# A one-core decoder step: single first blocks, squares through PSUM, a convolution in two chains, a mean from two products, and other groups for transferred lo parts

## Chip, core and metric

The kernel runs on one core of one Trainium2 chip, in one launch. The metric is device time in microseconds (us), the lower the better, given as the median of several executions. The core has a matrix engine (PE), a vector engine (DVE), an activation engine (ACT), a general engine (POOL) and a queue engine (SP) that issues most of the DMA transfers. Each runs its own list of instructions in a fixed order and waits on semaphores for the others.

## What is computed

One layer of a decoder trunk over 288 token columns: 256 of a prompt and 8 requests with 4 new tokens each. The width is 2048, the inner width 8192, everything is float32.

```python
h = rmsnorm(x, norm1_g)
proj = h @ w_in + b_in                      # 2048 -> 3 * 1024
a, gate, z = split(proj)
u = a * sigmoid(gate)
c = silu(layernorm(depthwise_causal_conv(hist_conv ++ u, conv_w) + conv_b))   # 31 taps
d = multiscale_pool(hist_pool ++ z)         # window means of 2, 4, 8, 16, less z
p = (d grouped @ pool_w) * pool_scale       # 4 groups of 256
x = x + concat(c, p) @ w_out
x = x + square(relu(rmsnorm(x, norm2_g) @ w_ff1)) @ w_ff2
y = rmsnorm(x, norm_f)
```

The last 30 values of u and the last 15 of z are outputs as well.

## The kernel before

**Layout and products.** Channels lie on the 128 partitions, tokens along the free axis. Each float32 operand is split into a rounded `hi` and the rest `lo`, and every product is three matmuls of 128x128 by 128x288: hi·hi (L297), hi·lo (L298), lo·hi (L299), in `gemm` (L283). 384 blocks of 128x128 of `w_in`, 16 of the pooling weights, 256 of `w_out` and 2 x 1024 of the feed-forward weights go through it, some 8,100 matmuls in all.

**Weights.** SP loads 512 KB at a time into `wr` (six buffers, L149), one such half being four blocks of rows for 256 columns. `split_part` (L251) makes `whi` on ACT (L257) and `wlo` in one of three ways, named by a letter: V is a subtraction on DVE (L262), G two subtractions on POOL (L265), and D is a negated copy on ACT (L259) followed by a second transfer of the same weights from memory that adds onto it (L260, issued by POOL). The letters of a group come from the table `WAYS` (L70): four letters for the four halves of a convolution tile `c0` to `c7` or of a pooling group `p0` to `p3`. `whi` and `wlo` have five buffers each.

**Order.** `SEQUENCE` (L45) is c0 c1 c2 c3 c4 p3 c5 p2 P3 c6 p1 P2 p0 P1 c7 P0, a capital letter being the small product of a pooling group. Python only fixes dependencies and priorities; a scheduler orders each engine's list from its own timing model. `later()` (L108) lowers the priority of what it encloses, `tc.issue_after(i)` puts an instruction behind another.

**The first stage.** Tiles c0 and c1 go first and together, so that each block of rows of x feeds 12 matmuls. `FIRST` (L183) lists the transfers: blocks 0 and 1 singly, the other 14 in pairs; six entries are issued ahead. For each entry `first_split` (L316) scales x by the gain on ACT, takes its lo part on DVE (L322), and splits the weights (way V). The RMS norm's squares (`squares`, L363) are made between these on ACT into a scratch of five 128x576 pieces in `z_all`, added on DVE (L372 to L374). `first_sums` puts their sum over the partitions (`pt`, L222) in PE's list ahead of block 15, `rsqrt_sums` (L213) takes the root on DVE and ACT, and `first_rows` has PE spread the result (L242) ahead of block 2 of c2.

**Convolution.** `conv_pair` (L392) evicts a tile's two banks into u and then writes, at low priority, the taps: for the prompt ACT makes tap 0 (L412) and DVE adds taps 1 to 30 one on the other in a PSUM tile `pc` (L415), shared by two tiles, the last into `c`. For the samples POOL multiplies all taps (`prd`, L419) and DVE reduces (L421).

**Pooling.** `pool_group` (L429) evicts z, POOL doubles the windows (L444), DVE and POOL take the mean less z (L449, L453), and ACT and DVE split the result `d` into `dx` (L455, L456). `pool_products` (L461) multiplies it and leaves scaled hi and lo parts (L467, L468).

**Layer norm and output.** `w_out` runs eight groups over the pooling half, then eight over the convolution half. Into the first eight are put, by `BETWEEN` (L530): the mean over channels (`ln_mean`, group 4, block 4: DVE adds the last pair of tiles and the two halves, L507 and L508, then one product with `ones`, L510), the squared deviations (`ln_sums`, group 5, block 6) and the rows (`ln_rows`, group 6, block 4). POOL has added the first three pairs before (L424). The outputs of u and z leave by SP at the lowest priority (L500, L501).

Of the kernel before, what the change touches and what calls it, by code (L numbers as in the profile page):

```python
# [69 lines left out]
WAYS = {"c2": "GVGV", "c3": "GDGD", "c4": "GDGD", "p3": "GDDG", "c5": "GDGD", "c": "GGGV", "p": "GVVG", "w": "GG", "ff": "VV"}  # L70
# [13 lines left out]
def trunk_kernel(ctx: ExitStack, tc: tile.TileContext, io):  # L84
# [95 lines left out]
    def first_x(k, n):  # L180
        nc.sync.dma_start(xT[:, k : k + n, :], io["xT"][:, k : k + n, :])
# [4 lines left out]
    for k, n in FIRST[:6]:  # L186
        first_x(k, n)
        if k > 0:
            first_weights(k, n, nc.sync)
# [124 lines left out]
    hx, firsts = [], []  # L314

    def first_split(k0, n):  # L316
        for k in range(k0, k0 + n):
            if k % 2 == 0:
                hx.extend(halves(act2("hx")))
            hh, hl = hx[k]  # L320
            nc.scalar.activation(hh, xT[:, k, :], AF.Copy, scale=v("norm1_g", k))
            nc.vector.scalar_tensor_tensor(out=hl, in0=xT[:, k, :], scalar=v("norm1_g", k), in1=f32(hh), op0=ALU.mult, op1=ALU.subtract)  # L322
# [5 lines left out]

    for j, (k, n) in enumerate(FIRST):
        if j >= 6:  # L330
            first_x(k, n)
            first_weights(k, n, nc.sync)
        first_split(k, n)
# [26 lines left out]
    scratch = z_all[:].rearrange("p k t -> p (k t)")[:, 0 : 5 * 2 * T].rearrange("p (n k t) -> p n k t", n=5, t=T)  # L360
    tot = [scratch[:, 0], scratch[:, 1]]

    def squares():  # L363

        nc.scalar.copy(scratch[:, :, :, 0:1], f32(firsts[0][0])[:, 1, 1, 0:10].rearrange("p (n k t) -> p n k t", n=5, t=1))
        for q in range(8):
            xq = xT[:, 2 * q : 2 * q + 2, :]
            a = q // 4
            dst = scratch[:, 2 + q % 3] if q % 4 else tot[a]
            nc.scalar.activation(dst, xq, AF.Square)  # L370
# [3 lines left out]
        nc.vector.tensor_tensor(tot[0][:, 0, :], tot[0][:, 0, :], tot[0][:, 1, :], op=ALU.add)  # L374
        return [tot[0][:, 0, :]]
# [4 lines left out]
    cs, pcs = [], []  # L380
    sum_c = tmpp.tile([P, 2, T], F32, name="sum_c", tag="ag2", bufs=2)
# [10 lines left out]
    def conv_pair(i, banks):  # L392
# [9 lines left out]
        for out, a, b in ((up[:, CH:UO], ta[:, :SEQ], tg[:, :SEQ]), (us[:, :, CH:US], samples(ta[:, SEQ:T], NS), samples(tg[:, SEQ:T], NS))):  # L402
            nc.vector.scalar_tensor_tensor(out=out, in0=a, scalar=v("b_in", i), in1=b, op0=ALU.add, op1=ALU.mult)
        if i % 2 == 0:
            cs.append(actp.tile([P, 2, T], F32, name=nm("c"), tag="c", bufs=4))
        c = cs[i // 2][:, i % 2, :]
        with later():
            if i % 2 == 0:
                pcs.append(cvp.tile([P, 2, SEQ], F32, name=nm("pc"), tag="cv"))
            pc = pcs[i // 2][:, i % 2, :]  # L410
            cwv = vec[:, CWO + i * CW : CWO + (i + 1) * CW]
            nc.scalar.activation(pc, up[:, 0:SEQ], AF.Identity, bias=v("conv_b", i), scale=cwv[:, 0:1])  # L412
            for w in range(1, CW):
                dst = pc if w < CW - 1 else c[:, 0:SEQ]
                nc.vector.scalar_tensor_tensor(out=dst, in0=up[:, w : w + SEQ], scalar=cwv[:, w : w + 1], in1=pc, op0=ALU.mult, op1=ALU.add)  # L415
# [6 lines left out]
            if i % 2 and 1 < i < N8 - 1:  # L422
                for m in range(2):
                    nc.gpsimd.tensor_tensor(sum_c[:, m, :], (cs[0] if i == 3 else sum_c)[:, m, :], cs[i // 2][:, m, :], op=ALU.add)  # L424
# [65 lines left out]
    conv_pair(1, pair1)  # L490
    conv_pair(2, third)
    for kind, i in SEQUENCE[3:]:
        if kind == "c":
            conv_pair(i, conv_products(i))
        elif kind == "p":
# [195 lines left out]
```

## Time and profile before

| | |
|---|---|
| median of 3 executions | 1104.44 us (1103.78 to 1106.19) |
| the profiled execution | 1105.06 us, of which the span from first to last instruction is 1103.1 us |
| granted PE clock, mean over the span | 0.996 |
| PE busy | 1087.3 us of the span, 8204 instructions |
| DVE, ACT, POOL busy | 638.2, 477.8, 179.1 us |
| HBM read, written | 185.68 MB, 4.28 MB |

The span falls into four stretches: the first stage with its loads (0 to about 31 us), the input projection with convolution and pooling (to about 172 us), the output projection (to about 290 us) and the feed-forward part. In a row of a group stand the line, the engine, what is written and read, the count, then busy time, mean duration in ns, the idle time of the engine ahead of it and what ended it. In a row of the timeline stand start, length, engine, line, operation, shapes, count, and in brackets the engine's idle time ahead of it and what ended that. A length with a count above one is from the first start to the last end. Matmuls overlap each other, so a matmul of 296 ns does not mean one result per 296 ns.

### The profile page before, as it was taken

To read this page: it belongs to the slowest core of one execution; us is meant where nothing else is said; L and a number is where in the kernel's file an instruction comes from. 1 tells how busy PE (TensorE), PEld (TensorE's weight loads), DVE (VectorE), ACT (ScalarE), POOL (GpSimd) and SP (SyncE) were. 2 spreads that over 40 slices of the span, in tenths; PEclk is the share of its full clock that TensorE was granted. 3 is DMA by queue.
4 is the path that set the end of the run, shared out by engine and by line. 5 is a ranking of instruction groups with operands and counts; after the bars stand their busy time and mean duration, and the time that the engine had idled before them with its cause. 6 is when DMAs were issued, how large, how long until landed. Compare 5 with 4: busy or idle time off the path is not lost.

```text
span 1103.1 us, 19716 instructions
## 1 busy us (share of the span) xinstructions
PE 1087.3 (99%) x8204; PEld 1085.0 (98%) x8204; DVE 638.2 (58%) x814; ACT 477.8 (43%) x585; POOL 179.1 (16%) x209
## 2 busy tenths in 40 slices
PE   9999999999999999999999999999999999999996
PEld 8999999999999999999999999999999999999996
DVE  7889999787555444445544444545544445554553
ACT  8654445565544433333443333444433334444441
POOL 0879989512000000000000000000000000000000
PEclk9999999999999999999999999999999999999998
DMA  9996568555555555555555555555555555555522
GB/s 334 279 275 176 155 159 245 168 169 162 166 161 170 168 162 168 171 161 165 170 167 162 171 163 165 171 168 161 169 170 160 168 171 164 165 170 163 164 75 86
DMA packets 58265, 191.24 MB, mean 173 GB/s; under 512 B 6208, under 2 KB 11328, under 8 KB 58176
## 3 DMA queue, kind: packets, MB, share of 16 engines
q1 hardware_dynamic: 56752, 185.53, 53.7%
q0 software_dynamic: 1152, 4.19, 2.1%
q8 instruction: 64, 1.05, 0.4%
q10 hardware_dynamic: 272, 0.26, 0.1%
q14 instruction: 25, 0.20, 0.0%
HBM read 185.68 MB, written 4.28 MB: 172 GB/s over the span
## 4 chain that ended last, share of the span: by engine, by line
PE 89%; DVE 8%; DMA 1%; issue 1%; ACT 1%; POOL 0%; SPq 0%; DVEq 0%; POOLq 0%
PE ac L297 30%; PE ac L299 30%; PE ac L298 29%; DVE pc L415 3%; DVE wlo L262 1%; DMA wlo<-in_w 1%; DVE xT L631 0%; DMA wr<-in_w 0%; DVE c L421 0%; POOL prd L419 0%; DVE q L521 0%; DVE dx L456 0%; DVE c L515 0%; PE pt L242 0%; DVE d L449 0%
## 5 line engine op out<-in xcount | busy, mean ns | idle before, releaser
L257 ACT CAST whi<-wr 128x1024 fp32r<-128x1024 f32 (+1 forms) x341 | 355.6, 1043 | 570.8 <-PE ac L298 537.1
L262 DVE TENSOR_TENSOR wlo<-wr,whi 128x1024 fp32r<-128x1024 f32 (+1 forms) x295 | 363.1, 1231 | 353.4 <-ACT whi L257 352.3
L297 PE MATMUL ac<-ax,whi 128*128 128x288 f32 x1024 | 303.2, 296 | 0.0
L297 PE MATMUL ac<-fx,whi 128*128 128x288 f32 x1024 | 303.1, 296 | 0.0
L299 PE MATMUL ac<-ax,wlo 128*128 128x288 f32 x1024 | 301.9, 295 | 0.0
L299 PE MATMUL ac<-fx,wlo 128*128 128x288 f32 x1024 | 301.9, 295 | 0.0
L298 PE MATMUL ac<-ax,whi 128*128 128x288 f32 x1024 | 298.5, 292 | 0.0
L298 PE MATMUL ac<-fx,whi 128*128 128x288 f32 x1024 | 298.5, 292 | 0.0
L298 PEld LDWEIGHTS ac<-fx,whi 128*128 128x128 f32 x1024 | 192.5, 188 | 0.0
L298 PEld LDWEIGHTS ac<-ax,whi 128*128 128x128 f32 x1024 | 192.5, 188 | 0.0
L297 PEld LDWEIGHTS ac<-ax,whi 128*128 128x128 f32 x1024 | 192.4, 188 | 0.0
L297 PEld LDWEIGHTS ac<-fx,whi 128*128 128x128 f32 x1024 | 192.4, 188 | 0.0
L299 PEld LDWEIGHTS ac<-ax,wlo 128*128 128x128 f32 x1024 | 191.5, 187 | 0.0
L299 PEld LDWEIGHTS ac<-fx,wlo 128*128 128x128 f32 x1024 | 191.5, 187 | 0.0
L297 PE MATMUL ac<-hx,whi 128*128 128x288 f32 x384 | 113.4, 298 | 1.3 <-ACT whi L257 1.3
L299 PE MATMUL ac<-hx,wlo 128*128 128x288 f32 x384 | 110.9, 295 | 1.0 <-DMA wlo<-in_w 0.8
L298 PE MATMUL ac<-hx,whi 128*128 128x288 f32 x384 | 111.4, 292 | 0.0
L265 POOL TENSOR_TENSOR wlo<-wr,whi 128x512 fp32r<-128x512 f32 x76 | 103.8, 1413 | 37.0 <-ACT whi L257 35.5
L415 DVE SCALAR_TENSOR_TENSOR pc<-u_all,vec,pc 128x256 f32<-128x256 f32 x232 | 99.7, 481 | 3.5 <-ACT pc L412 2.3
L297 PEld LDWEIGHTS ac<-hx,whi 128*128 128x128 f32 x384 | 72.3, 189 | 1.7 <-ACT whi L257 1.7
L299 PEld LDWEIGHTS ac<-hx,wlo 128*128 128x128 f32 x384 | 71.2, 188 | 1.5 <-DMA wlo<-in_w 1.0
L298 PEld LDWEIGHTS ac<-hx,whi 128*128 128x128 f32 x384 | 72.2, 188 | 0.0
(117 smaller groups left out, 826.8 us busy)
## 6 DMA issues: line engine op xcount, KB each, us to landing
wr<-in_w SPq DMA_DIRECT2D x335, 512.0 KB, 3.8
wlo<-in_w POOLq DMA_DIRECT2D x8, 512.0 KB, 7.3
xT<-in_xT SPq DMA_DIRECT2D x7, 288.0 KB, 8.0
wr<-in_w SPq DMA_DIRECT2D x5, 256.0 KB, 3.7
out_u_out<-u_all SPq DMA_DIRECT2D x1, 1208.0 KB, 8.6
out_yT<-xT SPq DMA_DIRECT2D x2, 576.0 KB, 2.9
u_all<-in_hist_c SPq DMA_DIRECT2D x8, 136.0 KB, 5.4
out_z_out<-z_all SPq DMA_DIRECT2D x1, 668.0 KB, 9.1
```

Of the source, the lines that this page charges most:

```text
L257: nc.scalar.copy(hi, raw)
L262: nc.vector.tensor_tensor(lo, raw, f32(hi), op=ALU.subtract)
L265: nc.gpsimd.tensor_tensor(lo[:, j : j + 2, :], raw[:, j : j + 2, :], f32(hi[:, j : j + 2, :]), op=ALU.subtract)
L297: nc.tensor.matmul(b, wh, xh, start=k == 0, stop=False)
L298: nc.tensor.matmul(b, wh, xl, start=False, stop=False)
L299: last = nc.tensor.matmul(b, wl, xh, start=False, stop=k == n - 1)
L415: nc.vector.scalar_tensor_tensor(out=dst, in0=up[:, w : w + SEQ], scalar=cwv[:, w : w + 1], in1=pc, op0=ALU.mult, op1=ALU.add)
```

## The change

It has eight parts.

1. `FIRST` lists four single blocks, then pairs; seven entries are issued ahead; block 1 of x goes by ACT's queue behind the first weights.
2. `squares` writes q = 1 to 7 into a one-buffer PSUM tile (`sq`, in the tag that `pt` also uses) and keeps one running total; each square and each add is put behind the conversion of block 2q + 3 on its engine.
3. A convolution tile's taps have their own function, called after `conv_pair` (for c0 and c1 after both evictions). ACT makes taps 0 and 1; DVE adds the even taps on the one and the odd taps on the other, and one addition joins them. `pc` holds one tile instead of two, in the same two PSUM buffers.
4. `sum_c` is 128x288: POOL adds tiles c1 to c6 one by one, and the mean is two products, of `sum_c` and of c7.
5. The squared deviations go singly (128x288) through PSUM tiles and are added onto `sum_c`'s buffer.
6. In `WAYS`, c3 goes from GDGD to GGGV, p2 from GVVG to GDVG, c6 from GGGV to GGGD.
7. `ln_mean` moves from block 4 to 3 of its group, `ln_sums` from block 6 to 7.
8. The output of u is issued within the first chunk of the feed-forward part.

```diff
-WAYS = {"c2": "GVGV", "c3": "GDGD", "c4": "GDGD", "p3": "GDDG", "c5": "GDGD", "c": "GGGV", "p": "GVVG", ...}
+WAYS = {"c2": "GVGV", "c4": "GDGD", "p3": "GDDG", "c5": "GDGD", "p2": "GDVG", "c6": "GGGD", "c": "GGGV", "p": "GVVG", ...}
...
-    FIRST = [(0, 1), (1, 1)] + [(k, 2) for k in range(2, KT, 2)]
+    FIRST = [(k, 1) for k in range(4)] + [(k, 2) for k in range(4, KT, 2)]
+    AHEAD = 7
     first_weights(0, 1, nc.scalar)
+    first_x(1, 1, nc.scalar)
...
-    scratch = z_all[:]...[:, 0 : 5 * 2 * T]...
-    tot = [scratch[:, 0], scratch[:, 1]]
+    tot = z_all[:]...[:, 0 : 2 * T]...
     def squares():
-        nc.scalar.copy(scratch[:, :, :, 0:1], ...)
         for q in range(8):
-            dst = scratch[:, 2 + q % 3] if q % 4 else tot[a]
-            nc.scalar.activation(dst, xq, AF.Square)
-            if q % 4:
-                nc.vector.tensor_tensor(tot[a], tot[a], dst, op=ALU.add)
-        nc.vector.tensor_tensor(tot[0], tot[0], tot[1], op=ALU.add)
+            dst = ms("sq")[:, :, :T] if q else tot
+            behind = [tc.issue_after(i) for i in converted[min(2 * q + 3, KT - 1)]]
+            with behind[0]:
+                nc.scalar.activation(dst, xq, AF.Square)
+            if q:
+                with behind[1]:
+                    nc.vector.tensor_tensor(tot, tot, dst, op=ALU.add)
...
-            nc.scalar.activation(pc, up[:, 0:SEQ], AF.Identity, bias=v("conv_b", i), scale=cwv[:, 0:1])
-            for w in range(1, CW):
-                dst = pc if w < CW - 1 else c[:, 0:SEQ]
-                nc.vector.scalar_tensor_tensor(out=dst, in0=up[:, w : w + SEQ], ..., in1=pc, ...)
+            nc.scalar.activation(pc[:, 0, :], up[:, 0:SEQ], AF.Identity, bias=v("conv_b", i), scale=cwv[:, 0:1])
+            nc.scalar.activation(pc[:, 1, :], up[:, 1 : 1 + SEQ], AF.Copy, scale=cwv[:, 1:2])
+            for w in range(2, CW):
+                part = pc[:, w % 2, :]
+                dst = c[:, 0:SEQ] if w == CW - 2 else part
+                nc.vector.scalar_tensor_tensor(out=dst, in0=up[:, w : w + SEQ], ..., in1=part, ...)
+            nc.vector.tensor_tensor(c[:, 0:SEQ], c[:, 0:SEQ], pc[:, 0, :], op=ALU.add)
...
-            if i % 2 and 1 < i < N8 - 1:
-                for m in range(2):
-                    nc.gpsimd.tensor_tensor(sum_c[:, m, :], ...)
+            if 0 < i < N8 - 1:
+                nc.gpsimd.tensor_tensor(sum_c, cs[0][:, 0, :] if i == 1 else sum_c, c, op=ALU.add)
...
     def ln_mean():
-        nc.vector.tensor_tensor(sum_c, sum_c, cs[-1], op=ALU.add)
-        nc.vector.tensor_tensor(sum_c[:, 0, :], sum_c[:, 0, :], sum_c[:, 1, :], op=ALU.add)
-        return nc.tensor.matmul(norm["mean"], ones, sum_c[:, 0, :], start=True, stop=True)
+        nc.tensor.matmul(norm["mean"], ones, sum_c, start=True, stop=False)
+        return nc.tensor.matmul(norm["mean"], ones, cs[-1][:, 1, :], start=False, stop=True)
...
-    BETWEEN = {4: {4: ln_mean}, 5: {6: ln_sums}, 6: {4: ln_rows}}
+    BETWEEN = {4: {3: ln_mean}, 5: {7: ln_sums}, 6: {4: ln_rows}}
```

Where the scheduler puts the instructions differs too. In the changed list POOL makes both parts of c3's second half ahead of c0's sample taps, issues p2's second transfer between the window sums of p3 and c6's fourth after the lo parts of c6's third; PE meets P3's small product some 60 matmuls later. On ACT the sixth square comes behind the cast of the last first-stage weights and the seventh behind the cast of c2's first half.

More of the change, by code (lines that the diff above doesn't have):

```diff
@@ L506, in ln_mean @@
     def ln_mean():
[L507 to L508 removed]
         norm["mean"] = ms("pmean")[:, 0, :T]
[L510 removed]
+        nc.tensor.matmul(norm["mean"], ones, sum_c, start=True, stop=False)
+        return nc.tensor.matmul(norm["mean"], ones, cs[-1][:, 1, :], start=False, stop=True)
     def ln_sums():
[L513 removed]
+        ssc = sum_c
         for c in cs:
             nc.vector.tensor_tensor(c, c, norm["mean"][:, None, :].to_broadcast([P, 2, T]), op=ALU.subtract)
[L516 to L523 removed]
+            for m in range(2):
+                first = m == 0 and c is cs[0]
+                q = ssc if first else cvp.tile([P, 512], F32, name=nm("q"), tag="cv")[:, :T]
+                nc.scalar.activation(q, c[:, m, :], AF.Square)
+                if not first:
+                    nc.vector.tensor_tensor(ssc, ssc, q, op=ALU.add)
+        norm["sums"] = rsqrt_sums([ssc], 1.0 / DC, AF.Silu)
         return norm["sums"][2]
```

58 lines of the change are left out of this document (27 added, 31 removed).

## Prediction

> **What bounds the kernel now.** I read the page first, then the busy time by stretch (length; busy time of PE, its weight loads, DVE, ACT and POOL; clock, DMA share, GB/s), then what PE waited for.
>
> ```profile
> span 1103.1 us, 19716 instructions
> PE 1087.3 (99%) x8204; PEld 1085.0 (98%) x8204; DVE 638.2 (58%) x814; ACT 477.8 (43%) x585; POOL 179.1 (16%) x209
> ```
>
> ```profile
> 107.00:150.00 43.00, 43.00 (x328) 43.00 (x327) 42.37 (x81) 20.86 (x32) 40.19 (x40) 1.00 0.51 154
> ...
> 296.00:1088.00 792.00, 792.00 (x5992) 792.00 (x5991) 379.51 (x362) 310.28 (x340) 0.00 (x0) 1.00 0.51 161
> ```
>
> ```profile
> PE ac L297 <- ACT whi L257: 1.3, 1, 1.3
> PE pmean L510 <- DVE sum_c L508: 1.3, 1, 1.3
> PE warm L203 <- DVE ones L193: 1.0, 1, 1.0
> PE ac L299 <- DMA wlo<-in_w: 0.8, 1, 0.8
> PE pp L297 <- DVE dx L468: 0.4, 1, 0.4
> PE pt L222 <- DVE q L522: 0.3, 1, 0.3
> PE ac L299 <- DVE wlo L262: 0.2, 1, 0.2
> ```
>
> PE is the bound. In the long last stretch it never idles and starts a matmul every 792 / 5992 = 0.132 us at granted clock 1.00. The change takes no weight product away, so it can only win waits: 1.3 + 1.3 + 0.8 + 0.4 + 0.3 + 0.2 = 4.3 us idle, the `ones` wait aside, which comes before any weight is there. Behind a wait the next matmul comes 0.24 us later instead of 0.132 (10.52 and 10.76 in the rows of the start below), about 0.1 us more for each of six: **4.9 us is the most to be had**, 0.45%. On the other side, DVE and POOL are almost full from 107 to 183 us (42.37 and 40.19 of 43), so work put on POOL there is not free.
>
> **First blocks.** Timeline of the start:
>
> ```profile
> 5.44 0.54 ACT L321 ACTIVATE hx<-xT,vec 128x288 fp32r<-128x288 f32 x1 [0.55 <-DMA xT<-in_xT]
> 6.67 0.62 ACT L257 CAST whi<-wr 128x512 fp32r<-128x512 f32 x1 [0.69 <-DMA wr<-in_w]
> 8.29 1.24 ACT L370 ACTIVATE z_all<-xT 128x576 f32<-128x576 f32 x2
> 9.29 0.38 SPq L178 DMA_DIRECT2D wr<-in_w  x1
> 9.44 1.03 ACT L257 CAST whi<-wr 128x1024 fp32r<-128x1024 f32 x1
> 10.52 0.40 PE L297 MATMUL ac<-hx,whi 128*128 128x288 f32 x1 [1.32 <-ACT whi L257]
> 10.76 0.29 PE L298 MATMUL ac<-hx,whi 128*128 128x288 f32 x1
> ```
>
> Block 1's weights land at 6.67. For the pair 2 and 3 ACT first makes two squares and casts from 9.44; the changed list puts the first square behind two single casts. Eight transfers are in flight on SP, and the issue at 9.29 waits, by its semaphore, for the landing of that pair, so the pair landed just before 9.29: 2.6 us for 800 KB behind block 1. Single blocks of 400 KB, at that rate, land at 8.0 and 9.3, or at 10.2 if their shorter rows go at the 210 KB/us of block 1 (256 KB from x1's landing, 5.44, to 6.67). PE leaves block 1 at 9.1 and needs 12 x 0.132 = 1.6 us per block: block 2 is cast at 8.6, no wait; block 3 is needed at 10.7 and cast at 9.9 to 10.8. Blocks 4 and 5 then land 2.1 us after block 3 and take a 1.03 us cast: 12.4 to 13.3, needed at 12.3. Before, PE began block 4 at 10.52 + 24 x 0.132 + 0.2 (the last wait above) + 0.2 for two restarts = 14.1. So PE is 0.8 to 1.7 us earlier at block 4, or not at all if the loads stay behind. The two more transfers on each side carry the same bytes.
>
> The Trainium skill, "DMA: Bandwidth & Descriptors", section "Issuing engines are not separate DMA queues", holds that transfers from any engine's queue share the same 16 engines, and a second issuer only saves issue time. By that, x1 on ACT's queue is worth at most one issue, which is less than the range just given; no run here shows it yet.
>
> **Squares.** The gain has to pass the first sums:
>
> ```profile
> 26.14 1.05 ACT L257 CAST whi<-wr 128x1024 fp32r<-128x1024 f32 x1 [0.97 <-DMA wr<-in_w]
> 27.73 1.43 DVE L374 TENSOR_TENSOR z_all<-z_all 128x288 f32<-128x288 f32 x1
> 31.64 0.59 PE L222 MATMUL pt<-ones,z_all 128*96 128x1 f32 x6
> 34.70 0.16 DVE L235 SCALAR_TENSOR_TENSOR st<-st 96x3 f32<-96x3 f32 x1
> 35.32 0.80 PE L242 MATMUL pt<-ident,st 96*128 96x96 f32 x6
> ```
>
> The sum is ready at 29.2, 2.4 us ahead of PE. In the changed list square 7 stands behind c2's first cast (26.14 to 27.2): square 0.7, add 0.7, halves 1.43, so 30.0 to 30.7. PE, if 0.8 to 1.7 us earlier, comes at 29.9 to 30.8. So the stage can keep about 0.9 us: **-0.9** (0 to -1.9).
>
> **Taps.** DVE's rows late in the projection, and the mean:
>
> ```profile
> 163.35 4.39 DVE L415 SCALAR_TENSOR_TENSOR pc<-u_all,vec,pc 128x256 f32<-128x256 f32 x11
> 174.79 2.06 DVE L415 SCALAR_TENSOR_TENSOR pc<-u_all,vec,pc 128x256 f32<-128x256 f32 x5 [0.82 <-ACT pc L412]
> 189.97 4.68 DVE L415 SCALAR_TENSOR_TENSOR pc<-u_all,vec,pc 128x256 f32<-128x256 f32 x9
> 197.43 1.14 DVE L507 TENSOR_TENSOR sum_c<-sum_c,c 128x576 f32<-128x576 f32 x1
> 198.60 1.41 DVE L508 TENSOR_TENSOR sum_c<-sum_c 128x288 f32<-128x288 f32 x1
> 200.06 0.75 PE L510 MATMUL pmean<-sum_c,ones 128*128 128x288 f32 x2 [1.28 <-DVE sum_c L508]
> 200.44 0.51 PE L297 MATMUL ac<-dx,whi 128*128 128x288 f32 x1
> 200.79 0.29 PE L298 MATMUL ac<-dx,whi 128*128 128x288 f32 x1
> ```
>
> Where two tiles alternate, 11 taps take 4.39 us, (4.39 - 0.48) / 10 = 0.39 each; where c7 stands alone, 9 take 4.68, (4.68 - 0.49) / 8 = 0.52: each waits for the one before. c7 pays 0.13 us on its last 24 or so taps, 3 us, which two chains take away, and L507 and L508 (2.6 us to 200.01) go. But in the changed list c6 has some 16 taps left when c7 begins, 6 us. 45 taps x 0.39 + 5 us of other rows behind 174.8 give c7 by 197.4 at the latest; when DVE is no longer behind in the evictions before, some 5 us sooner. PE reaches block 3 at 200.06 - 1.28 - 0.8 = 198.0, and what is won earlier moves both: the wait goes, **-1.4** with its restart (0 to -1.4). The second product adds PE work: from 200.06 to 200.79 pass 0.73 us for what takes 0.132 without the product, so **+0.6**.
>
> The wait ahead of `pp` (L468 queued behind a late L456) goes with DVE's backlog, **-0.5** (0 to -0.5). For `pt` in the layer norm, moved one block (0.8 us) back, the adds of 288 columns follow the four subtractions; L522 (1.45 us) goes; **-0.4** (0 to -0.4). Rows then come 31 matmuls, 4.1 us, behind the sums instead of 39; the root took 34.86 - 31.64 = 3.2 us in the first stage, so it fits with 0.9 us left: 0.
>
> **Groups.**
>
> ```profile
> 48.34 1.14 POOL L260 DMA_DIRECT2D wlo<-in_w  x1
> 54.03 1.43 POOL L260 DMA_DIRECT2D wlo<-in_w  x1
> 57.84 0.40 PE L299 MATMUL ac<-hx,wlo 128*128 128x288 f32 x1 [0.79 <-DMA wlo<-in_w]
> DMA to landing us min/median/max: 5.5/7.3/9.5
> 109.94 5.07 POOL L265 TENSOR_TENSOR wlo<-wr,whi 128x512 fp32r<-128x512 f32 x4
> L424 POOL TENSOR_TENSOR sum_c<-c,c 128x288 f32<-128x288 f32 x2 | 1.6, 807 | 0.0
> 160.95 3.62 POOL L265 TENSOR_TENSOR wlo<-wr,whi 128x512 fp32r<-128x512 f32 x2 [1.32 <-ACT whi L257]
> 165.02 2.56 POOL L265 TENSOR_TENSOR wlo<-wr,whi 128x512 fp32r<-128x512 f32 x2
> ```
>
> c3's fourth half, D, lands 9.5 us after its issue and PE waits: now it is V. **-0.9** (0 to -0.9). POOL gains one G, two subtractions, 2.56 us, in a stretch where it runs some us ahead of PE, and two more sums of 0.8. Where it may hurt: c4's first D, issued near 54 as before and needed 48 matmuls behind 57.84, at 64.2 less what is won; c6's new D, which POOL issues behind the four subtractions of 109.94, at 114 to 116, landing 5.5 to 7.3 us later, and needed 492 matmuls behind 57.84, at 122.8 less what is won; and the first `w_out` lo part, done at 167.58, just when PE is there, with two sums ahead of it now instead of one, inside an idle 1.32 us. I take **+0.6** for the three (0 to +3.5, each late by up to a little over 1 us). The output of u moves away from a place where nothing waited: 0.
>
> **The sum:** -0.9 - 1.4 + 0.6 - 0.5 - 0.4 - 0.9 + 0.6 = -2.9 us. The profiled execution took 1105.06, 2.0 more than its span: it would take 1102.2. It lies 0.6 above the median of the runs shown (1104.44); from that median the forecast is 1101.5.
>
> **Rivals.**
>
> *Lo parts come late instead.* POOL at 40 of 43 us and D's spread of 5.5 to 9.5 speak for it, the lookahead of several us ahead of most halves against. At +3.5 instead of +0.6: 1104.4.
>
> *The squares hold PE: slower.* `sq` has one buffer, so a square waits for the last add, and casts stand behind squares on ACT. If cast 1.03, scaling 0.96, square 0.67 and add 0.75 run one behind the other, a pair takes 3.4 us where PE needs 24 x 0.132 = 3.2, and the last two squares with their adds and the 1.43 follow at the end: `pt` at about 36 instead of 31.64, the rows 4.4 us late. Without the front's 0.9: -2.9 + 0.9 + 4.4 = +2.4, 1106.8. It decides from `pt` after about 33.6, where it eats the other 2.0 us. Against it: an add has a whole pair of time before the next square.
>
> *Two chains win nothing.* If the 0.39 of alternating taps came from their being of two tiles, c7's last 13 taps would still cost 0.52, 1.7 us more, and c6 and c7 would end by 199.1 instead of 197.4 at the latest, PE being there at 198.0: a wait of 1.1 us stays, 1102.6. The row of 11 taps at 0.39 speaks against it. The Trainium skill, "VectorE: DVE Perf Modes", section "The DRAIN you can't avoid", says that the next DVE operation waits until the pipe is empty, chained or not; by that rule two chains in one tile could save nothing, and the 0.39 beside operations of 0.48 disagrees with it.
>
> *All is kept.* The front gives 1.9 instead of 0.9 and POOL costs nothing: 1101.5 - 1.0 - 0.6 = 1099.9.
>
> **How the numbers follow.** Forecast 0.48 (own range 1100.2 to 1103.0), late lo parts 0.20, squares 0.14, no gain from chains 0.08, all kept 0.10. About 0.2% (2.2 us) is what a measurement of this kernel can tell from no change: below 1102.2 faster, above 1106.6 slower. Most of the forecast (0.37), a little of the chains (0.03) and all of the last are faster: 0.50. Slower: most of the squares' (0.12) and the end of the late lo parts (0.05), 0.17. The rest, 0.33, is the same. The range must take in the late lo parts and half of the squares' case: 1099.2 to 1106.8.
>
> **What would show it.** After: no PE wait on `whi` of 1.3 us near 10; `pt` near 30.7; no wait on a transferred `wlo` near 57; taps of one tile 0.39 apart; two products of the mean with no wait. I am wrong if PE waits for `pt` or on `wlo` for over 1 us, or if taps stay at 0.52.

## The result and the profile after

The changed kernel takes **1108.57 us** (median of 10 executions, 1107.38 to 1109.79), the kernel before, measured beside it, 1105.37 (1103.78 to 1109.81): a ratio of 1.0026, 95% interval 1.0014 to 1.0037. It is slower, by 3.2 us; the forecast was 1101.5. The profiled execution took 1109.79, span 1108.0, so it is the slowest of the ten, 1.2 us above their median.

First the page, and the busy time by stretch (columns as before: length; busy time of PE, its weight loads, DVE, ACT and POOL; clock, DMA share, GB/s).

```profile
span 1108.0 us, 19744 instructions
PE 1089.3 (98%) x8206; PEld 1087.0 (98%) x8206; DVE 633.5 (57%) x815; ACT 481.1 (43%) x597; POOL 179.1 (16%) x213
```

```profile
107.00:150.00 43.00, 40.74 (x309) 40.51 (x308) 40.31 (x70) 22.13 (x35) 36.10 (x40) 1.00 0.57 159
```

PE is still the bound, but between 107 and 150 us, where it never idled before, it now stands for 2.3 us, and DVE, which was full, has 11 instructions fewer in the same stretch. What PE waited for:

```profile
PE pp L301 <- DVE dx L465: 3.5, 2, 2.3
PE ac L302 <- POOL wlo L268: 1.5, 1, 1.5
PE warm L206 <- DVE ones L196: 1.0, 1, 1.0
PE pmean L521 <- DVE c L425: 0.9, 1, 0.9
PE ac L302 <- DMA wlo<-in_w: 0.9, 1, 0.9
PE ac L300 <- ACT hx L324: 0.6, 1, 0.6
PE ac L300 <- DVE xT L548: 0.2, 1, 0.2
```

The waits on `whi` near 10, on c3's transferred half and on `pt` are gone. In their place stand two on `pp`, 3.5 us, one on a POOL lo part, 1.5, one on c4's transferred half, 0.9, and the mean's, 0.9. To see where each counts, take the start of the n-th weight product in both profiled executions (both have 8112) and subtract. (The small products of the pooling groups stand elsewhere in the changed list, P3's some 60 places later, so the n-th is not the same block everywhere; the count is the same.)

| product | 1 | 49 | 193 | 385 | 433 | 841 | 865 | 1153 | 1177 | 1201 | 1225 | 1393 | 1441 | 1513 | 1801 | last |
|---|---|---|---|---|---|---|---|---|---|---|---|---|---|---|---|---|
| start before, us | 4.9 | 14.2 | 33.7 | 60.9 | 67.2 | 121.1 | 124.3 | 162.4 | 165.6 | 169.0 | 172.9 | 195.5 | 203.8 | 214.9 | 253.0 | 1088.6 |
| after minus before, us | +0.88 | -0.16 | -0.16 | -1.41 | -0.33 | -0.29 | +2.22 | +2.23 | +3.70 | +5.11 | +4.37 | +4.51 | +4.64 | +4.15 | +4.26 | +5.06 |

Read it as steps. The start wins 0.2 us, c3's half 1.1, which c4's half gives back at once. At 121 to 124 us **2.5 us are lost in one place**, then 1.5 and 1.4 near 165 to 169. Between products 1201 and 1225 it wins 0.7: the wait on `pp` that the kernel before has at 172.16 is gone. The mean comes out even (+0.13) and the layer norm's `pt` wins 0.5. The 0.8 us behind product 1801 lie where no line was edited, and they are not chance: every profile of a kernel built on the changed one has 0.79 or 0.80 there (e1, e3 to e8, e10, e11), those built on the kernel before (e2, e12) have 0.00. In each of 30 groups of products that read `ax` (L300, L302) three starts stand 139 to 145 ns behind the one before, where the kernel before has 126 to 132. What causes it was not tested.

The place of the 2.5 us, on PE, then DVE, then POOL:

```profile
123.54 0.40 PE L301 MATMUL pp<-dx,whi 128*128 128x288 f32 x1 [2.26 <-DVE dx L465]
```

```profile
117.02 6.46 DVE L465 TENSOR_TENSOR dx<-d,dx 128x576 fp32r<-128x576 f32 x1 [2.66 <-ACT dx L464]
```

```profile
114.55 0.86 POOL L263 DMA_DIRECT2D wlo<-in_w  x1
115.21 1.06 POOL L433 TENSOR_TENSOR sum_c<-sum_c,c 128x288 f32<-128x288 f32 x1
115.98 1.97 POOL L453 TENSOR_TENSOR s<-z_all 128x422 f32<-128x422 f32 x2
117.68 2.75 POOL L268 TENSOR_TENSOR wlo<-wr,whi 128x512 fp32r<-128x512 f32 x2
120.18 1.00 POOL L433 TENSOR_TENSOR sum_c<-sum_c,c 128x288 f32<-128x288 f32 x1
120.95 1.91 POOL L453 TENSOR_TENSOR s<-s 128x420 f32<-128x420 f32 x2
```

A subtraction on DVE with both inputs in SBUF (the same line, L456 in the trace of before, took 0.75 to 1.70 us) lasts 6.46 us. It ends 0.6 us after the last of POOL's run, which began with c6's new transfer, at 114.55, and ended at 122.86. All of DVE's queue stood behind it. In e3 and e4, which keep the transfer, the same instruction takes 6.56 and 6.46 us.

### The profile page after: what moved, and what is told of

Same layout as the page of the kernel before. It is cut to its first block, busy times and chain, and to the rows that moved or that the text cites. A ratio compares the mean times of both kernels' runs of the same rounds, so it can differ in the third digit from the quotient of the medians.

```text
span 1108.0 us, 19744 instructions
## 1 busy us (share of the span) xinstructions
PE 1089.3 (98%) x8206; PEld 1087.0 (98%) x8206; DVE 633.5 (57%) x815; ACT 481.1 (43%) x597; POOL 179.1 (16%) x213
## 4 chain that ended last, share of the span: by engine, by line
PE 90%; DVE 6%; DMA 1%; issue 1%; ACT 1%; POOL 0%; DVEq 0%; SPq 0%; POOLq 0%; ACTq 0%
PE ac L300 30%; PE ac L302 30%; PE ac L301 30%; DVE pc L424 3%; DMA wlo<-in_w 1%; DVE wlo L265 1%; DVE xT L643 0%; DMA xT<-in_xT 0%; DVE d L458 0%; DVE dx L465 0%; DVE dx L477 0%; PE pt L245 0%; ACT whi L260 0%; DVE c L431 0%; PE idle L228 0%
## 5 line engine op out<-in xcount | busy, mean ns | idle before, releaser
L300 PE MATMUL ac<-fx,whi 128*128 128x288 f32 x1024 | 303.1, 296 | 0.0
L300 PE MATMUL ac<-ax,whi 128*128 128x288 f32 x1024 | 302.9, 296 | 0.0
L302 PE MATMUL ac<-ax,wlo 128*128 128x288 f32 x1024 | 302.0, 295 | 0.0
L302 PE MATMUL ac<-fx,wlo 128*128 128x288 f32 x1024 | 301.9, 295 | 0.0
L300 PEld LDWEIGHTS ac<-ax,whi 128*128 128x128 f32 x1024 | 192.4, 188 | 0.0
L300 PEld LDWEIGHTS ac<-fx,whi 128*128 128x128 f32 x1024 | 192.4, 188 | 0.0
L302 PEld LDWEIGHTS ac<-ax,wlo 128*128 128x128 f32 x1024 | 191.9, 187 | 0.0
L302 PEld LDWEIGHTS ac<-fx,wlo 128*128 128x128 f32 x1024 | 191.5, 187 | 0.0
L300 PE MATMUL ac<-hx,whi 128*128 128x288 f32 x384 | 113.3, 299 | 0.6 <-ACT hx L324 0.6
L302 PE MATMUL ac<-hx,wlo 128*128 128x288 f32 x384 | 110.7, 296 | 0.9 <-DMA wlo<-in_w 0.9
L268 POOL TENSOR_TENSOR wlo<-wr,whi 128x512 fp32r<-128x512 f32 x78 | 104.6, 1393 | 39.4 <-ACT whi L260 39.2
L424 DVE SCALAR_TENSOR_TENSOR pc<-u_all,vec,pc 128x256 f32<-128x256 f32 x224 | 94.3, 481 | 5.5 <-POOL wlo L268 2.5
L300 PEld LDWEIGHTS ac<-hx,whi 128*128 128x128 f32 x384 | 72.6, 190 | 0.9 <-ACT hx L324 0.9
L302 PEld LDWEIGHTS ac<-hx,wlo 128*128 128x128 f32 x384 | 71.5, 189 | 1.1 <-DMA wlo<-in_w 1.1
```

Of the source, the lines that this page charges most:

```text
L268: nc.gpsimd.tensor_tensor(lo[:, j : j + 2, :], raw[:, j : j + 2, :], f32(hi[:, j : j + 2, :]), op=ALU.subtract)
L300: nc.tensor.matmul(b, wh, xh, start=k == 0, stop=False)
L302: last = nc.tensor.matmul(b, wl, xh, start=False, stop=k == n - 1)
```

## Experiments

Two theories for the 5.0 us of the `pp` and POOL waits. **A (lock-out):** c6's transfer makes POOL's next instructions follow so closely that DVE's subtraction can't start among them; PE waits for it, and DVE's backlog makes the later waits. **B (too much work):** six sums on POOL instead of two, the adds of the chains on DVE and one more POOL half make both late, whatever the transfer does. For the small gain at the start, for the mean and for the squares there were theories of their own. The kernels of one block below shared a chip with each other and with the kernel before, so the ratio compares best.

| kernel | median, us (executions: range) | before beside it | ratio (95%) |
|---|---|---|---|
| e1 changed, no transfer in c6 | 1104.71 (11: 1103.62 to 1105.88) | 1105.64 | 0.9991 (0.9983 to 1.0000) |
| e2 before, with c6's transfer | 1110.92 (5: 1110.35 to 1113.36) | 1105.64 | 1.0056 (1.0044 to 1.0069) |
| e3 changed, x1 on SP | 1108.90 (6: 1107.94 to 1111.44) | 1105.64 | 1.0034 (1.0021 to 1.0046) |
| e4 changed, longer warm-up | 1108.22 (8: 1107.52 to 1108.74) | 1105.64 | 1.0024 (1.0014 to 1.0033) |
| e5 e1, second chain of c7 in its own tile | 1103.64 (11: 1102.89 to 1105.12) | 1106.50 | 0.9975 (0.9964 to 0.9985) |
| e6 e1, one chain | 1104.28 (11: 1103.63 to 1105.12) | 1106.50 | 0.9978 (0.9969 to 0.9987) |
| e7 e1, mean two blocks later | 1103.28 (10: 1102.96 to 1104.52) | 1106.50 | 0.9973 (0.9964 to 0.9982) |
| e8 e1, old squares | 1102.52 (8: 1102.05 to 1107.90) | 1106.50 | 0.9984 (0.9967 to 1.0002) |
| e10 e1 again | 1104.85 (12: 1104.18 to 1105.74) | 1106.89 | 0.9983 (0.9973 to 0.9993) |
| e11 e1, old squares, one chain | 1101.20 (6: 1100.85 to 1101.67) | 1106.89 | 0.9950 (0.9937 to 0.9963) |
| e12 before, first blocks alone | 1103.20 (7: 1102.20 to 1103.75) | 1106.89 | 0.9967 (0.9956 to 0.9979) |

e9 is a measurement by itself and has no place in the table. On the second and third chip the kernel before scatters from 1103.80 to 1110.03, more than most of the others; what goes with it stands in the last section.

### c6's transfer: taken out of the changed kernel, put into the kernel before

```
e1   -"c6": "GGGD",                 (in WAYS of the changed kernel: c6 is GGGV again)
e2   +"c6": "GGGD",                 (in WAYS of the kernel before)
```

> The changed kernel without the transferred lo part of group c6 (its fourth half is again subtracted on DVE); all else as changed. Theory A (lock-out): the transfer that POOL issues at 114.55 lets seven POOL instructions follow back to back, and DVE's subtraction with two SBUF inputs (L465, 6.46 us instead of 0.75) can't start among them; PE then waits 2.3 us for pp, and DVE's backlog of some 3.5 us beyond PE's delay causes the waits of 1.2 and 1.5 us near 167 and 172. Then no DVE subtraction takes over 2.5 us here, no pp wait near 123, and the time falls from 1108.6 by 2.5 to 5 us: 1103.6 to 1106. Theory B (too much for POOL and DVE whatever the transfer does: six sums instead of two, the adds of two chains, one more POOL half): the waits near 167 and 172 stay, and the 1.2 us that go back to DVE make them longer: 1107 to 1109.

> The kernel before with one thing of the change: group c6's fourth lo part transferred instead of subtracted on DVE. Theory A (lock-out by what follows a transfer on POOL): a DVE subtraction with two SBUF inputs near 115 to 123 takes over 3 us, PE waits 1 to 3 us for pp soon after, and the time rises from 1105.4 to 1106.5 to 1109. Theory B (POOL's and DVE's added work is what costs): DVE has 1.2 us less to do, and the time stays at 1105.4 or falls by up to 1.

One entry of a table is worth 3.9 us in the one direction (1108.57 to 1104.71) and 5.3 in the other (1105.64 to 1110.92). Both speak for theory A and against B, which had DVE relieved by the transfer: in e1 DVE got 1.2 us more to do, none of its subtractions takes over 2.4 us, and PE waits for `pp` no more. The subtraction that took 6.46 us, and e1's longer waits, without the start's on `ones`:

```profile
115.75 1.45 DVE L465 TENSOR_TENSOR dx<-d,dx 128x576 fp32r<-128x576 f32 x1
```

```profile
PE pmean L521 <- DVE c L425: 1.5, 1, 1.5
...
PE ac L302 <- POOL wlo L268: 0.5, 1, 0.5
```

So the 1.2 us near 167 are gone, and of the 1.5 near 172 there is 0.5 left: most of those waits was the backlog. In e2 another line meets the same fate, behind the same transfer (DVE and POOL in one timeline; then PE, then DVE again, later):

```profile
117.34 0.88 POOL L260 DMA_DIRECT2D wlo<-in_w  x1
118.00 2.00 POOL L444 TENSOR_TENSOR s<-z_all 128x422 f32<-128x422 f32 x2
119.70 2.79 POOL L265 TENSOR_TENSOR wlo<-wr,whi 128x512 fp32r<-128x512 f32 x2
120.11 5.15 DVE L262 TENSOR_TENSOR wlo<-wr,whi 128x1024 fp32r<-128x1024 f32 x1
...
122.20 1.97 POOL L444 TENSOR_TENSOR s<-s 128x420 f32<-128x420 f32 x2
```

```profile
126.88 0.40 PE L299 MATMUL ac<-hx,wlo 128*128 128x288 f32 x1 [1.34 <-DMA wlo<-in_w]
```

```profile
200.80 5.30 DVE L507 TENSOR_TENSOR sum_c<-sum_c,c 128x576 f32<-128x576 f32 x1
```

L262 takes 1.21 us when it stands alone; here it takes 5.15. But the price came by other ways than I had written: PE does not wait for this subtraction, it waits 1.34 us for the transfer itself, and then 5.0 us at the mean for a second such instruction, L507, 5.30 us beside four POOL subtractions, the last of a run of fifteen (186.77 to 205.49) with no transfer near. L507 took 1.14 us in the profile of before; that DVE's backlog brought it into this place is argued, not shown. The time is also above the 1106.5 to 1109 that theory A gave. (This profile is of the slowest of e2's five executions, 1113.36. Its start was 2.0 us behind that of before, and the granted clock in it is 0.5 from 13.04 to 16.45 us and again from 204.19 to 211.01, around the wait at the mean; so part of the 5.3 us is the clock.)

### What closes the gaps on POOL

e9 leaves the reference's work out and holds three kinds of trial, each three times: ACT makes `x`; POOL does seven subtractions of 128x512; two or three copies on ACT later DVE's one subtraction becomes ready.

```
one:       7 x gpsimd.tensor_tensor(g[j], x, b, subtract)
transfer:  gpsimd.dma_start(lo, w, accum_op=add), then the same seven
chain:     7 x gpsimd.tensor_tensor(g[j], g[j-1], b, subtract)
all:       vector.tensor_tensor(d, y, b, subtract)      # both inputs in SBUF
```

> This kernel computes nothing of the reference: three kinds of trial, three times each, in which a DVE subtraction of 128x512 with both inputs in SBUF becomes ready while POOL is in the second of seven subtractions of the same kind. In the kind named one the seven are independent and need nothing but what the first waits for; in transfer a transfer is issued on POOL just ahead of them; in chain each reads the result of the one before and so waits for its semaphore. Theory K (a transfer issued ahead is what closes the gaps): DVE's subtraction takes 0.7 us or up to 2 us in one and chain, and over 5 us in transfer only. Theory L (it is enough that POOL's next instruction has nothing to wait for): over 5 us in one and transfer, under 2.5 us in chain. Theory M (neither; chance or other load on the chip decides): no order by kind, or no lock-out at all.

The first trial of each kind (start, length, engine):

```profile
13.78 9.03 POOL L118 TENSOR_TENSOR one<-x,b 128x512 f32<-128x512 f32 x7 [13.34 <-ACT x L107]
15.04 1.78 DVE L125 TENSOR_TENSOR d_one<-y,b 128x512 f32<-128x512 f32 x1 [10.25 <-ACT y L122]
...
25.82 1.00 POOL L114 DMA_DIRECT2D lo<-in_w  x1 [3.01 <-ACT x L112]
26.56 8.84 POOL L118 TENSOR_TENSOR transfer<-x,b 128x512 f32<-128x512 f32 x7
27.48 8.48 DVE L125 TENSOR_TENSOR d_transfer<-y,b 128x512 f32<-128x512 f32 x1 [10.67 <-ACT y L122]
...
38.11 0.69 DVE L125 TENSOR_TENSOR d_chain<-y,b 128x512 f32<-128x512 f32 x1 [2.15 <-ACT y L122]
```

The other two of each kind repeat it: 1.77 and 1.78, 8.32 and 8.33, 0.69 and 0.69 us. They repeat its timing too: DVE's instruction starts in the kind one just as POOL's second begins, in transfer during the first, and in chain as the first ends, where there is a gap. Other arrivals were not tried. Within that, theory K holds three times out of three, against L: seven independent instructions alone leave DVE a place at the next boundary (it waits out the running one, 1.1 us, and does its own 0.69), and the same seven behind a transfer leave none. The records of POOL show the difference: in the kind transfer each begins 0.3 us before the one ahead of it ends, in the kind one 0.04. It is 0.23 to 0.30 behind the transfers of the changed kernel and of e2 that are shown above. But it is 0.03 in the run that kept L507 out in e2, so the overlap goes with the transfer and is not the whole cause.

The Trainium skill, "SBUF — State Buffer", section "Who interferes with whom", says that a DVE instruction with two SBUF inputs contends with a GpSimd instruction that reads SBUF, and that whichever comes second blocks until the first is done. By that rule the wait is one POOL instruction at most, as in the kind one (1.78 us); the 8.3 to 8.5 us behind a transfer are seven, which the page does not have.

### The start

```
e3   -    first_x(1, 1, nc.scalar)
     -        if k != 1:
     -            first_x(k, n)
     +        first_x(k, n)
e4   -    for j in range(9):        # products on constants ahead of block 0
     +    for j in range(11):
e12  the kernel before with FIRST, AHEAD and first_x of the change, nothing else
```

> The changed kernel with x1 issued by SP in its place between block 0 and block 1, as in the kernel before, instead of ahead of x0 on ACT's queue. Theory C (x1 takes bandwidth from x0): x0's conversion starts near 4.35 instead of 5.23, the first product at 4.9 instead of 5.8, PE runs at 0.132 us a product from about 6.3 instead of 10, and product 48 comes 0.7 to 1.6 us earlier than in the changed kernel; later waits keep part of it: 1107 to 1108 where the changed kernel takes 1108.6. Rival D (the order of the two transfers makes no difference, the rate of all loads does): the first product stays near 5.8 and the time at 1108.6.

> The changed kernel with 11 instead of 9 products on constants ahead of the first block, so that PE is busy until about 5.7, when x0 has nearly landed. Theory C2 (the idle 0.57 us from 5.25 to 5.82 is why the products come every 0.24 us until 10): the first product stays at 5.8, the full rate comes near 6.3, and product 48 comes 1 to 1.8 us earlier than in the changed kernel unless loads hold it; 1107 to 1108 in all. Rival (the half rate comes from the loads or from the single blocks themselves): still 0.24 us a product until near 10, no change of the time, 1108.6.

> The kernel before with the first blocks of the change alone (four single blocks, seven pieces ahead, x1 on ACT's queue). Theory C (PE reaches product 48 up to 1.8 us earlier when x0 lands in time, 0.2 earlier when it comes late and the half rate holds on): 1104 to 1105 where the kernel before takes 1105.5, unless the waits behind (c3's transferred half at 57.8, the mean at 200) take it back: then 1105.3 and a longer wait at one of these two.

The start of the changed kernel first, ACT and PE in one timeline:

```profile
5.23 0.96 ACT L324 ACTIVATE hx<-xT,vec 128x288 fp32r<-128x288 f32 x2 [0.92 <-DMA xT<-in_xT]
...
5.82 1.09 PE L300 MATMUL ac<-hx,whi 128*128 128x288 f32 x3 [0.57 <-ACT hx L324]
...
10.11 0.29 PE L302 MATMUL ac<-hx,wlo 128*128 128x288 f32 x1
```

x0 is there at 5.23 instead of 4.35, PE idles 0.57 us, and then starts a product every 0.24 us until 10, where it went over to 0.13 near 6.3 before. With two more products on constants (e4) there is no idle and PE is at 0.13 by 6.9. (x0 was earlier there too, its conversion starts at 4.61, but the first product waits for those on constants.)

```profile
4.61 1.49 PE L206 MATMUL warm<-ones 128*128 128x128 f32 x6
5.75 1.06 PE L300 MATMUL ac<-hx,whi 128*128 128x288 f32 x3
6.62 0.32 PE L301 MATMUL ac<-hx,whi 128*128 128x288 f32 x1
```

The 49th product comes 1.65 us before that of the kernel before, where it was 0.16 in the changed kernel. That is what theory C2 says, but it does not show it: this lead is 1.07 in e3 and 1.5 to 1.8 us in all other kernels with the change's start (e1, e5 to e8, e10 to e12), without a longer warm-up. The trace's record of the granted clock has the step. Full clock begins at 9.86 us in the changed kernel's profile, at 6.28 in that of before, at 6.67 in e4, and between 4.20 and 7.24 in all others. e1 and e10 have the start of the changed kernel to the letter, and full clock from 6.35 and 4.20. So the half rate until 10 belongs to this one profile of the changed kernel. In e10 and e12 idles of 0.93 and 0.56 us came after full clock had begun, and the products are 0.13 apart from 6.6; in the changed kernel the 0.57 came before it. In e8 one of 0.45 came before it too and full clock still began at 6.10. So the place and the length of the idle may decide; that is argued, not shown.

The next loads took 0.6 of the lead in most. In e3 x0 came at 4.33 again and the first product at 4.9, as theory C had it, but the lead is smaller than where x0 came late (PE waits 0.73 us for `whi` at product 49): the loads behind set the pace, and theory C's price falls. The whole times of e3 and e4, 1108.90 and 1108.22, lie within what the changed kernel scatters (1107.38 to 1109.79). In e3 the lead is gone before the lock-out: a wait of 1.18 us for c4's second transfer leaves 0.40 at product 841, where the changed kernel has 0.29. In e4 it is not the lock-out that eats it. Everything there comes 1.29 us earlier, POOL's run, the subtraction and `pp`:

```profile
115.73 6.46 DVE L465 TENSOR_TENSOR dx<-d,dx 128x576 fp32r<-128x576 f32 x1 [2.67 <-ACT dx L464]
```

```profile
122.25 0.40 PE L301 MATMUL pp<-dx,whi 128*128 128x288 f32 x1 [2.26 <-DVE dx L465]
```

Behind this wait the granted clock falls to one half for 3.41 us, which it does not do in the changed kernel, and e4 goes from 1.58 us ahead of the kernel before at product 841 to 2.48 behind at 865. The changed kernel loses 2.51 there, so some 1.5 of e4's 4.06 us are the clock. The stretch from 124 to 126 us, in e4 and then in the changed kernel (the clock is the third number from the end):

```profile
124.00:126.00 2.00, 2.00 (x10) 2.00 (x10) 2.00 (x6) 1.34 (x2) 0.21 (x1) 0.50 0.31 78
```

```profile
124.00:126.00 2.00, 2.00 (x17) 2.00 (x16) 2.00 (x4) 0.84 (x1) 0.00 (x0) 1.00 0.00 0
```

By themselves, on the kernel before, the first blocks are worth 0.33% (0.21 to 0.44), 3.7 us, which is more than theory C gave. The profile shows 2.2 of them: the lead of 1.10 us at product 193, and c3's wait, which is gone there too (the lead grows to 2.14 by product 385). The rest stays open. It would fit that the wait near 10 us, which the single blocks take away, brings a stretch of half clock in some executions of the kernel before; e2, which has the same start, shows one behind it, the one profile of the kernel before does not.

### Taps and mean

```
e5   if i == 7: the first 21 taps in one chain; from the 22nd on two, the second in a PSUM tile of its own
e6   one chain: for w in range(1, CW), all in pc[:, 0, :], no ACT start for the second, no closing add
e7   -    BETWEEN = {4: {3: ln_mean}, ...
     +    BETWEEN = {4: {5: ln_mean}, ...
     (all three without c6's transfer)
```

> The changed kernel without c6's transfer, and with the last convolution tile's second chain put in a PSUM tile of its own (the one that c6 leaves), begun at its 22nd tap; the first 21 go down the first chain, beside c6's. Theory E (each tap waits for the last instruction that touched its PSUM tile, so two chains in one tile still go one behind the other at 0.52 us, and the 0.39 of alternating taps came from two tiles): the last taps stand 0.39 apart, c7 ends about 1.3 us earlier than without this (11 taps times 0.13), the wait of 1.5 us ahead of the second product of the mean shrinks to 0.2 to 0.5, and the time falls from 1104.7 to 1103.4 to 1104.0. Rival F (0.52 is the cost of taps of one convolution tile, by the memory they read): the taps stay at 0.52 and the time at 1104.7.

> The changed kernel without c6's transfer and with one chain in each convolution tile: 30 taps one behind the other, no second start on ACT and no closing add on DVE. By theory E the second chain won nothing, so that the taps alone stay at 0.52, and the closing add (0.41) and its eight siblings go: 1104.2 to 1104.8 beside 1104.7. If two chains do save (0.13 us on some 11 taps that stand alone), the wait of the mean grows by over 1 us: 1105.7 or more.

> The changed kernel without c6's transfer and with the mean's products ahead of block 5 instead of block 3 of their output pair, 1.6 us later on PE. What theory G says (the mean's place is 1.5 us too early for c7's taps, and nothing behind it is in a hurry): the wait of 1.5 us goes, the sums behind it come at the same time as before while PE is earlier, and if they still come in time the kernel takes 1103.2 to 1103.6 instead of 1104.7. Rival H (the sums then hold PE): pt waits for about what the mean no longer does, and the time stays at 1104.5 to 1105.

c7's last taps in the changed kernel, with the two chains, and then in e5 with each chain in its own tile:

```profile
194.49 4.68 DVE L424 SCALAR_TENSOR_TENSOR pc<-u_all,vec,pc 128x256 f32<-128x256 f32 x9
```

```profile
194.62 2.05 DVE L432 SCALAR_TENSOR_TENSOR pc<-u_all,vec,pc 128x256 f32<-128x256 f32 x5
```

Nine taps in 4.68 us are (4.68 - 0.49) / 8 = 0.52 apart, to the digit what one chain had before. Five in 2.05 are (2.05 - 0.48) / 4 = 0.39. Theory E holds: with both chains in one tile, the program's semaphores make a tap of the one wait for the tap of the other just ahead of it. (In the instruction lists its wait names the instruction one back; with two tiles it names the one two back. Whether the tile counts there or the piece of PSUM that it fills was not tested.) e5 took 1.1 us off e1, and the wait of the mean went from 1.5 to 0.7. e6, without any second chain, is no slower than e1, and in its profile the second product of the mean waits for nothing; the gain that two chains were to bring is not there.

e7 takes 1.4 us off e1 with one number: the mean stands where c7 is done, nothing behind it gets late, theory G. e5 and e7 ran on another chip than e1; against the kernel before the three are 0.9975, 0.9973 and 0.9991, and 0.9983 where e1 ran again as e10. The intervals of the first two overlap that of e10, so the waits in the profiles show these gains better than the times.

### Squares

```
e8   squares() of the kernel before (three buffers in SBUF, no issue_after), without c6's transfer
e11  e8's squares and e6's one chain
```

> The changed kernel without c6's transfer and with the squares as in the kernel before (three buffers in SBUF, no order against the casts). Theory I (the squares were never late; PE reaches pt at 30.5 to 31.5 and the old sum was ready at 29.2): pt waits for nothing and the time stays at 1104.7, within 0.6. Rival J (the old squares stand ahead of the first casts and hold the start, as in the profile of the kernel before, where two of them came between block 1 and the pair behind it): PE waits 0.5 to 1.5 us for whi near 10 to 13 and the time is 1105.2 to 1106.

> The changed kernel without c6's transfer once more, as the base on the chip of the two beside it: 0.998 to 1.0 of the kernel before, about 1104.7.

> The changed kernel without c6's transfer, with the old squares and with one chain in each convolution tile, the version that the runs so far point to. Theory N (the new squares, one buffer and two of them behind c2's first casts, put the lo parts of the groups behind them later, the transferred ones among them; the old ones give that back, 1 to 2 us, and one chain costs nothing): 1102 to 1103 where the base takes 1104.7. Rival (the 1102.5 of the old squares was a matter of that chip, and three of its eight runs at 1105 to 1108 are the truer time): 1104 to 1106.

Neither theory of e8 had it: no wait near 10 to 13 came back, and yet five of its eight executions took 1102.05 to 1102.58 (the other three 1104.97 to 1107.90, unexplained; no profile shows one of them). Two profiles show a reason, on ACT and POOL around the root of the first sums. e10, new squares, by engine:

```profile
27.12 0.66 ACT L374 ACTIVATE sq<-xT 128x576 f32<-128x576 f32 x1 [1.03 <-DVE z_all L377]
27.71 1.04 ACT L260 CAST whi<-wr 128x1024 fp32r<-128x1024 f32 x1
31.34 0.21 ACT L232 ACTIVATE st<-st 96x3 f32<-96x3 f32 x1 [2.59 <-DVE st L231]
```

```profile
34.09 6.03 POOL L268 TENSOR_TENSOR wlo<-wr,whi 128x512 fp32r<-128x512 f32 x4 [3.05 <-ACT whi L260]
53.75 1.01 POOL L263 DMA_DIRECT2D wlo<-in_w  x1
```

and e8, old squares:

```profile
27.85 1.05 ACT L260 CAST whi<-wr 128x1024 fp32r<-128x1024 f32 x1 [2.06 <-DMA wr<-in_w]
29.90 1.05 ACT L260 CAST whi<-wr 128x1024 fp32r<-128x1024 f32 x1 [1.00 <-DMA wr<-in_w]
31.21 0.21 ACT L232 ACTIVATE st<-st 96x3 f32<-96x3 f32 x1 [0.26 <-DVE st L231]
```

```profile
31.03 2.55 POOL L268 TENSOR_TENSOR wlo<-wr,whi 128x512 fp32r<-128x512 f32 x2
34.89 5.24 POOL L268 TENSOR_TENSOR wlo<-wr,whi 128x512 fp32r<-128x512 f32 x4 [1.32 <-ACT whi L260]
51.86 1.06 POOL L263 DMA_DIRECT2D wlo<-in_w  x1 [0.53 <-ACT tg L404]
```

In ACT's list the root (31.2) stands behind a fixed number of casts. The new squares leave one cast fewer ahead of it: ACT then idles 2.59 us before the root, the cast comes behind it and the table load that follows, POOL idles 3.05 us for it, and c4's first transfer is issued 1.9 us later. In e10 PE waited 1.1 us for a transferred part, in e8 for none, and the mean's wait is gone with the backlog. e11, on the same chip as e10, is 3.65 us faster (1101.20 against 1104.85), as theory N had it and by more than its 1102 to 1103. PE's waits in e11 are two:

```profile
PE warm L206 <- DVE ones L196: 1.0, 1, 1.0
PE pp L300 <- ACT dx L463: 0.3, 1, 0.3
```

**e11 beats both kernels**: 0.9950 of the kernel before (0.9937 to 0.9963), span 1098.8. It keeps of the change the first blocks, the mean from two products, the layer norm's sums and the groups other than c6, and drops the new squares, the second chain and c6's transfer.

## Why the prediction was wrong

The forecast was -2.9 us; the profiled execution has +5.1, the median +3.2. Two of the signs that it named for being wrong came, a wait of 1.5 us on a POOL `wlo` and taps at 0.52. By its own steps:

- **Groups, the step that failed.** It says of c6's new transfer that POOL issues it at 114 to 116, that it lands 5.5 to 7.3 us later and is needed at 122.8, and books +0.6 (0 to +3.5) for it and two others as lo parts that come "late by up to a little over 1 us". It was issued at 114.55 and PE did not wait for it (in e2 it did, 1.34 us). The step put at nothing, without a reason, what a transfer on POOL does to the instructions queued behind it there, and by them to DVE: 2.5 us at once and most of 2.9 more near 165 to 169 as backlog (e1: 3.9 us in the median). The rest of the step held: c3's fourth half won 1.1 (-0.9 said), and c4's first transfer cost 1.1 at 63.87, within its "little over 1".
- **Taps.** "3 us, which two chains take away" was wrong: 0.52 apart as before. The rival that two chains win nothing was right, with its reason: 0.39 does come from two tiles, through the waits on the tile; its price was not tested, since the lock-out moved everything around it. The DRAIN rule weighed there (the Trainium skill, "VectorE: DVE Perf Modes", section "The DRAIN you can't avoid") has the next operation start when the pipe is empty, semaphore or not, which would leave no difference between 0.39 and 0.52; e5 shows both spacings of the same taps. The section adds that an operation that is not held starts earlier.
- **Mean.** -1.4 + 0.6 was said, +0.13 came: the second product cost its 0.6, and a wait of 0.93 stayed because c7 ended at 203.86, when PE was there. With the mean two blocks later (e7) the wait goes as forecast.
- **First blocks.** -0.9 was said, -0.16 came in this profile because of the half rate until 10; e12, e10 and e1, which have full clock earlier, have -1.1 at product 193, e11 -1.6. The term was about right, and that the profile missed it was bad luck; that PE's rate at the start can change was not seen. x1 on ACT's queue is worth nothing that e3 could show, as the Trainium skill, "DMA: Bandwidth & Descriptors", section "Issuing engines are not separate DMA queues", had it.
- **Squares.** Right that the first `pt` would not be late (it waits for nothing in any run), and the rival that squares hold PE did not occur. Missed: the cast that they push behind the root, which sets POOL back by some 2 us. The step asked only what PE waits for next, not what ACT's list does to POOL.
- **Behind the mean.** No term was written for the products on `ax`, whose 0.8 us belong to every kernel built on the changed one, e11 too; the step that left them out is the sum's silence on lines without an edit.
- **`pp` and layer norm.** -0.5 was said for the wait on `pp`, and it went, worth 0.7; two others on `pp`, 3.5 us, came as a consequence of the first point. The -0.4 for the layer norm's `pt` measured -0.47.

Late lo parts (1104.4, chance 0.20) was the nearest rival in kind, and too small, since it had POOL late for PE and not DVE locked by POOL. Nothing in the profile of before showed a lock-out; the nearest rows were DVE subtractions of up to 2.3 us beside POOL, which were taken for the worst there is.

## What to carry to other kernels

A transfer issued on POOL is not priced by its landing alone: look at what POOL has ready behind it, and at every DVE instruction with two SBUF inputs in that stretch, which may wait for the whole run. Chains of this kind that are to overlap need tiles of their own, not halves of one. When an instruction moves in an engine's list, ask which other engine is fed by what it pushes back; a gain at the start of a kernel counts only if nothing behind it takes it back, such as a transfer that lands late (e3) or a stretch of half clock behind a wait (e4).

## What the runs showed of the hardware that was not expected

- Behind a transfer issued on POOL, a run of ready POOL instructions keeps a DVE subtraction with two SBUF inputs out to its end: 8.48, 8.32 and 8.33 us in place of 0.69 in e9, 6.46 in the changed kernel, 5.15 in e2. A transfer ahead was enough for it in each of these; it is not needed each time, as L507 in e2 (5.30 us with none near) shows, and what else brings it stays open. So does the cause of e8's three longer executions.
- After an idle, PE may run at a product every 0.24 us for some 3.4 us, and may not. In e4 the wait of 2.26 us at 122.25 is followed by 0.24 from 122.7 to 126.1; the same wait in the changed kernel by one such step. The granted clock in the trace is 0.5 over these stretches: 122.72 to 126.13 in e4 and 13.04 to 16.45 in e2, 3.41 us each, and 204.19 to 211.01 in e2, twice that. In these records full clock lasts whole multiples of 3.413 us (34 of them in e4 up to 122.72, 320 in the changed kernel from 9.86), so each run has a grid of its own. In e4 the wait (119.99 to 122.25) lies within one piece of it; in the changed kernel a step of the grid, at 122.50, parts it (121.28 to 123.54) into 1.2 and 1.0 us. That this is why one lost its clock and the other did not fits both, and was not tested. At a start the record begins only with the full clock, and the column of the stretches gives 1.00 ahead of that, so there the distance between products tells. The Trainium skill, "TensorE: Matmul & The Clock Gate", section "What's actually happening", has a window of 3.4 us that runs freely and looks at how busy PE was; the lengths of 3.41 and 6.83 us agree with it.
- The longer executions of the kernel before go with a lower clock: of those measured beside e1 to e12, the ones under 1105.3 us have a mean granted clock of 0.996 to 0.998, those over 1108.5 us 0.993 or 0.994. Where in these executions it was lower no profile shows.
- Products of lines without an edit cost 0.8 us more in 30 places of the `ax` stretches, in every kernel built on the changed one and in none built on the kernel before; the cause stays open.
